# Early MLP-up products, per-tile right-hand sums, later turns and one moved output-projection tile in a two-layer decoder trunk

## The chip, the cores and the metric

One core of a Trainium2 chip runs the whole program in one launch. The metric is device microseconds of that core, the median of several executions. The engines are PE (TensorE), DVE (VectorE), ACT (ScalarE), POOL (GpSimd) and SP (SyncE, which here issues nearly all DMAs). Each takes its instructions in the order of the program.

## The reference

Two layers over 1024 tokens of width 1024, all in f32. Layer 0 mixes with NSA (compressed, selected and window attention), layer 1 with sliding-window attention and sinks (SWA). Each is followed by an MLP; each sublayer is normalised before and after, and modulated by vectors that come from c through `ada_w`.

```python
for i in range(DEPTH):                                   # DEPTH = 2
    mod = silu(c) @ ada_w[i] + ada_b[i]
    sh1, sc1, g1, sh2, sc2, g2 = split(mod, 6)
    h = modulate(rms_norm(x, norm_g[i, 0]), sh1, sc1)
    y = nsa_mixer(h, ...) if i % 2 == 0 else swa_sink_mixer(h, ...)
    x = x + (1 + g1) * rms_norm(y, norm_g[i, 1])
    h = modulate(rms_norm(x, norm_g[i, 2]), sh2, sc2)
    a = relu(h @ w_up)                                   # 1024 -> 4096
    y = (a * a) @ w_down                                 # 4096 -> 1024
    x = x + (1 + g2) * rms_norm(y, norm_g[i, 3])
```

## The kernel before, in words

An f32 product is made of three matmuls (lines 572 to 574): each operand is split into a high part (`wh`, `hh`, `oh`, hi of `wt`; ACT or DVE rounds it) and a low part (`wl`, `hl`, `ol`, lo of `wt`; one subtraction), and hi·hi, lo·hi and hi·lo are added in PSUM.

The order of the work is written out by hand: `spread` interleaves lists of steps, `go` runs them one by one, and after each step lets up to two entries of the list `behind` run whose delay has passed. `later(f, n)` puts an entry there with a delay of n steps, `chain` runs stages one step apart. The first entry holds back those behind it.

**Output projection.** For each of eight token tiles, `out_steps` loads the attention output `o` (in layer 0 two halves from HBM, added by DVE on L1727), splits it into `oh` and `ol`, and runs 48 matmuls; then come the gate, the norm (`yg`, `ms`, `r`, `x`), the store, and the next norm (`junk`, `ms`, `r`, `xr` on L472). `done` puts the turns behind, with a delay of DL = 4 steps. In layer 0 the eight tiles follow the attention; in layer 1 they are spread over the attention units.

**Turns.** `turn` transposes `xr` on PE (L1234), ACT puts it into the right operand `raw` (L1245) with scale and bias. Tiles 0 to 3 fill B11 and B21, tiles 4 to 7 fill B12 and B22 (two tiles of 128 x 2 x 512 each).

**MLP up.** h @ w_up goes by 2 x 2 blocks with 7 products in place of 8 (a Strassen scheme) for each of the 16 column pairs q. Products 1 and 2 need only B11 and B21 as right operands, from tiles 0 to 3; products 6, 5, 7, 3 and 4 need sums over all eight: T1 = B12 - B11, B22 - T1, T3 = B22 - B12 and B21 - (B22 - T1). So products 1 and 2 of the first PAIRS0 = 5 pairs run ahead (10 early products of 12 matmuls) while the last tile is normalised and the sums are made: six 128 x 1024 subtractions on POOL and two on DVE (L1257), then `split` of each right operand (ACT L1250, DVE L1251). `prep` makes the left operand `wt` of a product AHEAD = 3 products before it: hi on ACT (L1330), lo on POOL for the early ones and on DVE for the rest (L1331). The first early loads and preps (`lead`) are spread over the last output-projection tile. `load` takes early columns from the pool `raw`, which has three buffers and also serves the weights of the projections and `adaw`.

**Side work.** The modulation vectors are made by DVE from rows of `ada_w` (L323, one 512 KB load each) as side steps of the MLP and of the projections. The gate of layer 0's MLP, `ada_gate(0, 1)`, is a side of its MLP up.

All big tiles of this part (`hr`, `hh`, `hl`, `wt`, `u`, `x`) come from one pool of 41 slots.

Of the kernel before, what the change touches and what calls it, by code (L numbers as in the profile page):

```python
# [18 lines left out]
P = 128  # L19
# [12 lines left out]
PAIRS0 = 5  # L32
SIDE2 = 40
AHEAD = 3
DL = 4
# [57 lines left out]
class Trunk:  # L93
# [1127 lines left out]
    def up_setup(self, w_up, col):  # L1221
# [36 lines left out]

        def tile(t, xr):
            steps = [lambda c=c: (turn(t, xr, c), put(t, c)) for c in range(2)]  # L1260
            if t == 3:
                steps += [lambda c=c, j=j: split((1, 2)[c], raw[0, c, j]) for c in range(2) for j in range(2)]
            if t == 7:
                V, G = nc.vector, nc.gpsimd
                b11, b21, b12, b22, t1 = (lambda j, n=n: (*n, j) for n in ((0, 0), (0, 1), (1, 0), (1, 1), (2, 0)))
                steps.append(lambda: [minus(e, *f(j)) for f in (lambda j: (t1(j), b12(j), b11(j)), lambda j: (b11(j), b22(j), t1(j)))
                                      for j, e in ((0, V), (1, G))])
                steps += [lambda j=j: (split(6, raw[b11(j)]), minus(G, b12(j), b22(j), b12(j))) for j in range(2)]
                steps += [lambda j=j: (split(5, raw.pop(t1(j))), minus(G, b21(j), b21(j), b11(j)), raw.pop(b11(j))) for j in range(2)]
                for p, b in ((7, b12), (3, b22), (4, b21)):  # L1270
                    steps += [lambda p=p, b=b, j=j: split(p, raw.pop(b(j))) for j in range(2)]
            return steps
# [24 lines left out]
        def prep(i):  # L1297
# [10 lines left out]
            if p == 1:  # L1308
                r = w[11] if early else w[11]
# [21 lines left out]
            (nc.gpsimd if early else nc.vector).tensor_tensor(lo, r, hi.bitcast(F32), op=ALU.subtract)  # L1331
# [3 lines left out]

        def before(i):

            out = []
            n = i + AHEAD
            if 0 <= n < len(order):  # L1340
                out.append(lambda: prep(n))
            out += [lambda q=q: load(q, True) for q in range(2, PAIRS0) if n == 4 * (q // 2) + q % 2 - 3]
            for q in range(n_q):
                if n == at[q] - 2:
# [3 lines left out]
        lead = [lambda q=q: load(q, True) for q in range(2)] + [f for i in range(-AHEAD, 0) for f in before(i)]  # L1348
        return tile, (R, order, before, left, lead)

    def mlp_up(self, up, side, sd, begin):
# [70 lines left out]
        for i, (q, p) in enumerate(order):  # L1422
# [3 lines left out]
            (ramp if i < 2 * PAIRS0 else steps).extend(own)  # L1426
# [205 lines left out]
    def run(self):  # L1632
# [59 lines left out]
        side = self.ada_gate(0, 0) + self.ada_pre(0, 1)  # L1692
# [4 lines left out]
        for l in range(2):  # L1697
# [14 lines left out]
            def done(t, x, take=take, xr=xr):  # L1712
                def turn():
                    for k, f in enumerate(take(t, xr)):
                        self.later(f, DL if k == 0 else 1)
                self.chain(self.norm_stages(x, xr, t) + [turn])

            if l == 0:
# [11 lines left out]
                def more(n):  # L1730
                    return {26: loads[0:1], 27: loads[1:2], 28: loads[2:3], 29: loads[3:5], 30: loads[5:6], 31: loads[6:]}.get(n, [])

                self.nsa_attention(more, parts[-1][1][QN:])
                self.pe = self.w2 = self.Kc = self.Vc = self.cmask = self.fmask = self.gate = None
                outs = [self.out_steps(t, lambda t=t: load(t), src[t], gate, x1[t], done) for t in range(NT)]
                self.mark("wout")
                outs[0][0]()
                for t in range(NT):
                    steps = outs[t][1]
# [51 lines left out]
            side = self.ada_gate(0, 1, True) + self.ada_pre(1, 0, None, True) if l == 0 else self.ada_gate(1, 1, True)  # L1791
# [35 lines left out]
```

## Time and profile before

| | |
|---|---|
| median of 3 runs | 2559.97 us (2558.47 to 2565.79) |
| profiled execution | 2561.28 us; its span 2559.3 us; granted clock 0.972 |
| busy | PE 2396.3 us (94%), DVE 1946.4 (76%), ACT 1397.0 (55%), POOL 1274.1 (50%) |
| instructions on PE | 11974 matmuls |
| out-projection of layer 0 | PE from 793.4 to 888.7 us |
| layer 0's first product after the early ones | 933.70 us |
| layer 1's first product after the early ones | 1959.00 us |

A time in a row of the timeline is the start in the span, then the duration; what stands in brackets is the idle time of that engine before it and what ended that time. PE's matmuls overlap, so their rate is read from start to start.

### The profile page before, as it was taken

The numbers are of one execution on the slowest core, as the hardware profiler recorded it, in microseconds if no ns is written. First come the engines' busy times: TensorE is split into PE (matmuls) and PEld (weight loads), VectorE is DVE, ScalarE is ACT, GpSimd is POOL, SyncE is SP. The second block draws the span as 40 slices with busy tenths as digits, with TensorE's granted clock in tenths as the row PEclk, the third lists the DMA queues.
The fourth block names the chain that finished last, engine by engine and source line by source line (L and its number), as shares of the span: only waits on it lengthen the run. The fifth ranks groups of instructions, "written<-read, shape, count | busy, mean of one in ns | idle before, by whom it ended". The sixth has DMA issues, their size and how long they took to land.

```text
span 2559.3 us, 36576 instructions
## 1 busy us (share of the span) xinstructions
PE 2396.3 (94%) x11974; PEld 1996.3 (78%) x11974; DVE 1946.4 (76%) x3751; ACT 1397.0 (55%) x2959; POOL 1274.1 (50%) x1256
## 2 busy tenths in 40 slices
PE   6989899999998979999999999889787999999997
PEld 4789788888887867778778887767676788888886
DVE  7965479999895579888899777477647876787656
ACT  4632368898983544444444454378765454445433
POOL 4420566565662255334955613477545543494433
PEclk9999999999999989999999999989899999999999
DMA  7367623122227536555988564452223555587754
GB/s 277 116 220 243 215 79 96 39 90 66 72 67 165 148 127 215 197 185 181 359 312 309 203 215 148 124 157 68 65 67 120 201 170 179 179 308 251 228 185 171
DMA packets 237205, 436.08 MB, mean 170 GB/s; under 512 B 19204, under 2 KB 120792, under 8 KB 237016
## 3 DMA queue, kind: packets, MB, share of 16 engines
q1 hardware_dynamic: 208216, 404.39, 47.3%
q0 software_dynamic: 28800, 29.36, 4.7%
q8 instruction: 94, 1.54, 0.2%
q14 instruction: 95, 0.78, 0.1%
HBM read 319.38 MB, written 114.31 MB: 169 GB/s over the span
## 4 chain that ended last, share of the span: by engine, by line
PE 58%; DVE 16%; DMA 10%; issue 6%; POOL 4%; ACT 4%; SPq 1%; DVEq 0%; POOLq 0%; ACTq 0%
PE b L574 14%; PE b L573 14%; PE b L572 14%; PE b L880 5%; PE b L903 5%; PE o L925 4%; DMA adaw<-in_ada_w_dram 3%; DVE wt L1331 2%; DVE p L884 2%; DMA w<-in_mlp_w_up_dram 2%; DMA w<-in_nsa_w_in_dram 1%; DMA wr<-in_mlp_w_down_dram 1%; DVE u L1358 1%; DVE pT L910 1%; DVE ada L323 1%
## 5 line engine op out<-in xcount | busy, mean ns | idle before, releaser
L574 PE MATMUL b<-hh,wt 128*128 128x512 f32 x896 | 350.8, 395 | 25.1 <-POOL wt L1331 21.2
L572 PE MATMUL b<-hh,wt 128*128 128x512 f32 x896 | 354.4, 396 | 9.8 <-ACT wt L1330 9.8
L573 PE MATMUL b<-st,st 128*128 128x512 f32 x896 | 349.5, 390 | 5.4 <-DVE st L1477 5.4
L573 PE MATMUL b<-hl,wt 128*128 128x512 f32 x896 | 352.4, 393 | 0.0
L574 PE MATMUL b<-st,st 128*128 128x512 f32 x896 | 348.3, 389 | 0.0
L572 PE MATMUL b<-st,st 128*128 128x512 f32 x896 | 332.5, 390 | 1.6 <-DVE u L1358 1.6
L888 ACT ACTIVATE p<-p,nm 128x256 f32<-128x256 f32 (+7 forms) x384 | 251.2, 660 | 59.0 <-DVE nm L884 57.8
L1028 POOL TENSOR_SCALAR p<-p,rl,nsam 128x640 f32<-128x640 f32 (+7 forms) x256 | 200.4, 796 | 137.8 <-DVE rl L1026 96.8
L1477 DVE TENSOR_TENSOR st<-sr,st 128x1024 fp32r<-128x1024 f32 (+1 forms) x128 | 193.3, 1510 | 77.5 <-ACT st L1476 76.1
L1403 POOL TENSOR_TENSOR sx<-u,u 128x512 f32<-128x512 f32 x64 | 106.2, 1660 | 273.0 <-ACT u L1371 224.8
L910 DVE TENSOR_TENSOR pT<-b,pT 128x512 fp32r<-128x512 f32 (+1 forms) x334 | 215.4, 657 | 27.6 <-ACT pT L909 27.4
L574 PEld LDWEIGHTS b<-hh,wt 128*128 128x128 f32 x896 | 170.3, 190 | 66.1 <-POOL wt L1331 22.9
L1370 ACT ACTIVATE u<-u 128x512 f32<-128x512 f32 x128 | 80.6, 630 | 244.6 <-DVE u L1358 244.5
L909 ACT ACTIVATE pT<-b 128x512 fp32r<-128x512 f32 (+1 forms) x334 | 187.2, 580 | 43.1 <-PE b L903 36.9
L572 PEld LDWEIGHTS b<-hh,wt 128*128 128x128 f32 x896 | 170.3, 190 | 50.4 <-ACT wt L1330 15.9
L1476 ACT ACTIVATE st<-sr 128x1024 fp32r<-128x1024 f32 (+1 forms) x128 | 122.2, 955 | 158.8 <-PE b L573 104.8
L573 PEld LDWEIGHTS b<-st,st 128*128 128x128 f32 x896 | 168.2, 188 | 42.6 <-DVE st L1477 8.2
L903 PE MATMUL b<-ident,p 128*128 128x128 f32 x1296 | 195.9, 277 | 5.0 <-DVE nm L884 4.1
L1477 DVE TENSOR_TENSOR st<-wr,st 128x1024 fp32r<-128x1024 f32 (+1 forms) x128 | 181.8, 1420 | 20.8 <-ACT st L1476 18.1
L573 PEld LDWEIGHTS b<-hl,wt 128*128 128x128 f32 x896 | 170.0, 190 | 35.0
L572 PEld LDWEIGHTS b<-st,st 128*128 128x128 f32 x896 | 168.2, 188 | 37.3 <-DVE u L1358 2.3
L574 PEld LDWEIGHTS b<-st,st 128*128 128x128 f32 x896 | 168.2, 188 | 34.7
(276 smaller groups left out, 6183.6 us busy)
## 6 DMA issues: line engine op xcount, KB each, us to landing
adaw<-in_ada_w_dram SPq DMA_DIRECT2D x96, 512.0 KB, 4.7
sr<-s SPq DMA_DIRECT2D x96, 512.0 KB, 4.8
wr<-in_mlp_w_down_dram SPq DMA_DIRECT2D x96, 512.0 KB, 6.0
w<-in_mlp_w_up_dram SPq DMA_DIRECT2D x74, 512.0 KB, 4.2
s<-sx SPq DMA_DIRECT2D x64, 512.0 KB, 5.1
x<-x SPq DMA_DIRECT2D x48, 512.0 KB, 4.1
s<-u SPq DMA_DIRECT2D x64, 256.0 KB, 2.1
we<-in_mlp_w_down_dram SPq DMA_DIRECT2D x64, 256.0 KB, 4.0
```

The lines of the kernel that those rows point to most:

```text
L572: mm(out, s[0], m[0], start=first, stop=False)
L573: mm(out, s[0], m[1], start=False, stop=False)
L574: mm(out, s[1], m[0], start=False, stop=last)
L880: self.nc.tensor.matmul(out, q[:, g], k[z], start=z == 0, stop=z == 1)
L888: self.nc.scalar.activation(p, p, AF.Exp, scale=-1.0, bias=nm, accum_out=l)
L903: nc.tensor.transpose(pt[:, g * P:(g + 1) * P], p[:, cols], self.ident)
L909: nc.scalar.activation(x[:, 0, 0:w], pt[:, 0:w], AF.Copy)
L910: nc.vector.tensor_tensor(x[:, 1, 0:w], pt[:, 0:w], x[:, 0, 0:w].bitcast(F32), op=ALU.subtract)
L1028: nc.gpsimd.tensor_scalar(ps[g], ps[g], rl[:, g:g + 1], gate[:, g, b:b + 1], op0=ALU.mult, op1=ALU.mult)
L1403: nc.gpsimd.tensor_tensor(z[n][:, k], x, y, op=op)
L1476: nc.scalar.activation(hi, r, AF.Copy)
L1477: nc.vector.tensor_tensor(lo, r, hi.bitcast(F32), op=ALU.subtract)
```

## The change

1. PAIRS0 goes from 5 to 6: twelve early products. Their right operands are split in `lead`, their left operands by a schedule (`when`) that is ahead of the old one, and their lo is made by DVE. Loads of the early pairs from the fourth on go to slots.
2. T1 and T3 are made for each of tiles 4 to 7 by itself (`near`): two 128 x 2 x 128 subtractions on DVE and two on POOL. Only B22 - T1 (DVE) and B21 - that (POOL) are left for the end.
3. Turns of tiles 0 to 6 come 8 steps later in place of 4 and run one per step; `go` runs the first two entries that are due, wherever they stand.
4. In layer 0 the first output-projection tile stands in the last attention unit.
5. `ada_gate(0, 1)` is a side of the NSA projection (8 more loads and DVE steps there, 8 fewer in MLP up).

```diff
-PAIRS0 = 5
+PAIRS0 = 6
+TURN = 8
@@ go
-                if self.behind and self.behind[0][1] <= 0:
-                    self.behind.pop(0)[0]()
+                due = next((b for b in self.behind if b[1] <= 0), None)
+                if due:
+                    self.behind.remove(due)
+                    due[0]()
@@ up_setup
+        def near(t, j):
+            if t1(j) not in raw:
+                raw[t1(j)] = self.slot("hr", F32, [P, 2, 512])
+            v = lambda n: raw[n][:, :, (t - 4) * P:(t - 3) * P]
+            nc.vector.tensor_tensor(v(t1(j)), v(b12(j)), v(b11(j)), op=ALU.subtract)
+            nc.gpsimd.tensor_tensor(v(b12(j)), v(b22(j)), v(b12(j)), op=ALU.subtract)
...
-            if t == 3:
-                steps += [lambda c=c, j=j: split((1, 2)[c], raw[0, c, j]) for c in range(2) for j in range(2)]
+            if t > 3:
+                steps.append(lambda: (near(t, 0), near(t, 1)))
             if t == 7:
...
+                steps.append(lambda: [minus(V, b11(j), b22(j), t1(j)) for j in range(2)])
+                for p, b in ((6, b11), (5, t1), (7, b12), (3, b22)):
+                    if p == 5:
+                        steps.append(lambda: [minus(G, b21(j), b21(j), b11(j)) for j in range(2)])
+                    steps += [lambda p=p, b=b, j=j: split(p, raw[b(j)]) for j in range(2)]
+                steps += [lambda j=j: split(4, raw[b21(j)]) for j in range(2)]
...
-                r = self.raw_weight(self.raw, w_up, list(range(KT)), 2 * q * P, P)
+                r = self.raw_weight(self.raw if q < 3 else self.slot, w_up, list(range(KT)), 2 * q * P, P)
...
-            (nc.gpsimd if early else nc.vector).tensor_tensor(lo, r, hi.bitcast(F32), op=ALU.subtract)
+            nc.vector.tensor_tensor(lo, r, hi.bitcast(F32), op=ALU.subtract)
...
+        first = at[0]
+        when = lambda i: -1 if i < 3 else (i - 3) // 2 if i < first else max(i - first + 5, i - AHEAD) if i < first + 5 else i - AHEAD
...
+            out = [lambda n=n: prep(n) for n in range(len(order)) if when(n) == i]
+            if i in (0, 1, 2):
+                out += [lambda q=q: load(q, True) for q in (3 + i,) if q < PAIRS0]
...
+        lead = [lambda q=q: load(q, True) for q in range(3)] + [lambda j=j: split(1, raw[b11(j)]) for j in range(2)] + \
+            before(-1) + [lambda j=j: split(2, raw[b21(j)]) for j in range(2)]
@@ mlp_up
-            (ramp if i < 2 * PAIRS0 else steps).extend(own)
+            (ramp if i < 2 * PAIRS0 + 10 else steps).extend(own)
@@ run
-        side = self.ada_gate(0, 0) + self.ada_pre(0, 1)
+        side = self.ada_gate(0, 0) + self.ada_pre(0, 1) + self.ada_gate(0, 1)
...
-                    for k, f in enumerate(take(t, xr)):
-                        self.later(f, DL if k == 0 else 1)
+                    self.later(lambda: self.chain(take(t, xr)), DL if t == NT - 1 else TURN)
...
+                    if n == NT * 4 - 1:
+                        return spread(loads[6:], [outs[0][0], lambda: None, lambda: None] + outs[0][1][:8])
...
-            side = self.ada_gate(0, 1, True) + self.ada_pre(1, 0, None, True) if l == 0 else self.ada_gate(1, 1, True)
+            side = self.ada_pre(1, 0, None, True) if l == 0 else self.ada_gate(1, 1, True)
```

**Place A: PE at the end of layer 0's attention.** PE before (`o` is the attention's output in PSUM, `b` a PSUM bank, `oh` and `ol` the operand of out-projection tile 0):

```order
L925 MATMUL o_9617<-pT_9713,kv_7926 128x512
L925 MATMUL o_9617<-pT_9723,kv_7926 128x512
L572 MATMUL b_9764<-wh_8498,oh_9741 128x512
L573 MATMUL b_9764<-wl_8499,oh_9741 128x512
L572 MATMUL b_9795<-wh_9212,oh_9741 128x512
L573 MATMUL b_9795<-wl_9213,oh_9741 128x512
L574 MATMUL b_9764<-wh_8498,ol_9742 128x512
```

PE now, at the start of the last unit's weighting:

```order
L906 MATMUL b_9689<-ident,p_9545 128x128
L928 MATMUL o_9679<-pT_9640,kv_7754 128x512 x2
L575 MATMUL b_9700<-wh_8475,oh_9652 128x512
L576 MATMUL b_9700<-wl_8476,oh_9652 128x512
L906 MATMUL b_9707<-ident,p_9567 128x128
L906 MATMUL b_9707<-ident,p_9583 128x128
L906 MATMUL b_9723<-ident,p_9567 128x128
L906 MATMUL b_9723<-ident,p_9583 128x128
L906 MATMUL b_9707<-ident,p_9593 128x128
L906 MATMUL b_9723<-ident,p_9593 128x128
L928 MATMUL o_9679<-pT_9663,kv_7754 128x512
L577 MATMUL b_9700<-wh_8475,ol_9653 128x512
```

The 48 matmuls of tile 0 have moved in between the transposes (L906) and the weighting (L928) of the last unit; tile 1's follow directly after the unit.

SP at the same place, before (`o_5`, `o_6`: stores of the attention's output of tiles 5 and 6; `o_0`: the loads for tile 0):

```order
L1122 DMA o_5_2938<-otmp_9427 128x512
L547 DMA w_10471<-in_mlp_w_up_dram 128x8x128
L1122 DMA o_6_2939<-otmp_9619 128x512
L547 DMA w_10487<-in_mlp_w_up_dram 128x8x128
L1726 DMA o_9734<-o_0_2933 64x8x128 x2
L1726 DMA o_9735<-o_0_2933 64x8x128 x2
```

SP now:

```order
L1125 DMA o_5_2984<-otmp_9396 128x512
L1740 DMA o_9645<-o_0_2979 64x8x128 x2
L1740 DMA o_9646<-o_0_2979 64x8x128 x2
L550 DMA w_10522<-in_mlp_w_up_dram 128x8x128
L1125 DMA o_6_2985<-otmp_9668 128x512
L1186 DMA x_9656<-in_x_dram 128x1024
L1171 DMA gbc_9786<-gate_811 128x1024
L550 DMA w_10545<-in_mlp_w_up_dram 128x8x128
L1740 DMA o_9860<-o_1_2980 64x8x128 x2
L1740 DMA o_9861<-o_1_2980 64x8x128 x2
```

The loads of tile 0 stand ahead of the store of `o_6`; those of tile 1 stand behind the load `w_10545`.

**Place B: POOL at the start of layer 0's MLP up.** POOL before (`r` is the norm's factor of a tile, `wt` a left operand, `hr` a right one):

```order
L451 TENSOR_TENSOR r_10661<-ms_10660,mhalf 128x1
L1331 TENSOR_TENSOR wt_10684<-w_10582,wt_10684 128x512
L1257 TENSOR_TENSOR hr_10725<-hr_10424,hr_9919 128x1024
L1257 TENSOR_TENSOR hr_10421<-hr_10432,hr_10421 128x1024
L1257 TENSOR_TENSOR hr_9919<-hr_10435,hr_10725 128x1024
L1257 TENSOR_TENSOR hr_10424<-hr_10435,hr_10424 128x1024
L1257 TENSOR_TENSOR hr_9927<-hr_9927,hr_9916 128x1024
L1331 TENSOR_TENSOR wt_10734<-w_10547,wt_10734 128x512
L1257 TENSOR_TENSOR hr_9930<-hr_9930,hr_9919 128x1024
L1331 TENSOR_TENSOR wt_10780<-w_10582,wt_10780 128x512
```

POOL now:

```order
L1270 TENSOR_TENSOR hr_10441<-hr_10464,hr_10441 128x2x128
L454 TENSOR_TENSOR r_10650<-ms_10649,mhalf 128x1
L454 TENSOR_TENSOR r_10711<-ms_10710,mhalf 128x1
L1270 TENSOR_TENSOR hr_10438<-hr_10461,hr_10438 128x2x128
L1270 TENSOR_TENSOR hr_10441<-hr_10464,hr_10441 128x2x128
L1260 TENSOR_TENSOR hr_10011<-hr_10011,hr_9990 128x1024
L1260 TENSOR_TENSOR hr_10014<-hr_10014,hr_9993 128x1024
L1418 TENSOR_TENSOR sx_11114<-u_10702,u_11014 128x512
```

No `wt` is left on POOL, and of six large subtractions two are left.

**Place C: PE at a turn in layer 1's attention.** PE before (`o`: weighting, L880: scores, L903: transposes of p, `xr`: the normalised tile):

```order
L574 MATMUL b_18653<-wh_17478,ol_18577 128x512
L925 MATMUL o_18649<-pT_18569,V_16476 128x512
L1234 MATMUL b_18666<-ident,xr_18633 128x128 x4
L1234 MATMUL b_18675<-ident,xr_18633 128x128 x4
L880 MATMUL b_18684<-K_16472,qs_18586 128x256 x4
L880 MATMUL b_18685<-K_16472,qs_18586 128x256 x4
L903 MATMUL b_18708<-ident,p_18355 128x128 x4
```

PE now:

```order
L577 MATMUL b_18667<-wh_17492,ol_18591 128x512
L883 MATMUL b_18680<-K_16486,qs_18600 128x256 x4
L883 MATMUL b_18681<-K_16486,qs_18600 128x256 x4
L906 MATMUL b_18704<-ident,p_18351 128x128 x4
L928 MATMUL o_18663<-pT_18583,V_16490 128x512
L1237 MATMUL b_18732<-ident,xr_18647 128x128 x4
L906 MATMUL b_18741<-ident,p_18351 128x128 x4
L928 MATMUL o_18749<-pT_18636,V_16489 128x512 x2
```

Eight score matmuls and four transposes stand ahead of the turn that stood behind it, and the turn's two halves are a step apart.

## Rows read from the trace of the kernel before

**Rows 1.** The page, part 4: shares of the chain that ended last, by engine.
```profile
PE 58%; DVE 16%; DMA 10%; issue 6%; POOL 4%; ACT 4%; SPq 1%; DVEq 0%; POOLq 0%; ACTq 0%
```

**Rows 2.** Stretch of 50 us: busy of each engine, granted clock, DMA share, GB/s.
```profile
900.00:950.00 50.00, 37.12 (x143) 28.64 (x142) 42.46 (x38) 26.25 (x41) 26.76 (x11) 0.86 0.38 120
```

**Rows 3.** Timeline of PE where layer 0's out-projection begins.
```profile
793.36 0.76 PE L572 MATMUL b<-wh,oh 128*128 128x512 f32 x1 [6.76 <-DVE oh L1179]
...
797.76 0.63 PE L574 MATMUL b<-wh,ol 128*128 128x512 f32 x1
798.18 0.63 PE L572 MATMUL b<-wh,oh 128*128 128x512 f32 x1
...
799.38 0.40 PE L573 MATMUL b<-wl,oh 128*128 128x512 f32 x1
799.62 0.39 PE L574 MATMUL b<-wh,ol 128*128 128x512 f32 x1
```

**Rows 4.** Chain of waits before that: start, duration, what.
```profile
782.29 8.77 DMA o<-o
791.19 1.24 DVE o L1727
792.51 0.70 DVE oh L1179
```

**Rows 5.** Timeline of PE at the start of layer 0's MLP up.
```profile
888.67 1.04 PE L1234 MATMUL b<-ident,xr 128*128 128x128 f32 x8
...
917.24 0.80 PE L574 MATMUL b<-hh,wt 128*128 128x512 f32 x1 [9.82 <-POOL wt L1331]
...
933.70 0.50 PE L572 MATMUL b<-hh,wt 128*128 128x512 f32 x1 [1.63 <-ACT wt L1330]
```

**Rows 6.** Timeline of POOL there.
```profile
899.97 14.99 POOL L1257 TENSOR_TENSOR hr<-hr,hr 128x1024 f32<-128x1024 f32 x5 [2.19 <-ACT hr L1245]
```

**Rows 7.** Timeline of DVE, before and in that stretch.
```profile
863.50 2.35 DVE L1251 TENSOR_TENSOR hl<-hr,hh 128x1024 fp32r<-128x1024 f32 x2
...
895.86 0.75 DVE L472 TENSOR_SCALAR xr<-x,r 128x1024 f32<-128x1024 f32 x1 [1.02 <-POOL r L451]
...
910.48 20.11 DVE L1251 TENSOR_TENSOR hl<-hr,hh 128x1024 fp32r<-128x1024 f32 x9 [3.33 <-ACT hh L1250]
```

**Rows 8.** Timeline of PE at the start of layer 1's MLP up.
```profile
1914.89 0.39 PE L572 MATMUL b<-hh,wt 128*128 128x512 f32 x1
...
1942.56 0.80 PE L574 MATMUL b<-hh,wt 128*128 128x512 f32 x1 [9.81 <-POOL wt L1331]
...
1959.00 0.50 PE L572 MATMUL b<-hh,wt 128*128 128x512 f32 x1 [1.64 <-ACT wt L1330]
```

**Rows 9.** Waits of PE from 1700 to 1915: total, times, longest.
```profile
PE b L1234 <- DVE xr L472: 17.1, 5, 5.1
```

**Rows 10.** Timeline of PE at one of these turns.
```profile
1774.16 1.18 PE L1234 MATMUL b<-ident,xr 128*128 128x128 f32 x8 [4.12 <-DVE xr L472]
1774.99 2.06 PE L880 MATMUL b<-K,qs 128*128 128x256 f32 x8
...
1779.40 1.10 PE L880 MATMUL b<-K,qs 128*128 128x256 f32 x8
```

**Rows 11.** Waits of PE from 940 to 1240 (MLP up of layer 0).
```profile
PE b L574 <- DVE wt L1331: 3.3, 3, 2.7
...
PE b L436 <- DVE adag L432: 2.9, 1, 2.9
```

**Rows 12.** Line L323 up to 300 us: durations in ns; what its engine waited for.
```profile
L323 DVE SCALAR_TENSOR_TENSOR ada<-adaw,cond,ada x21: 1264/1285/2316, 77.3 to 265.7; 128x1024 f32<-128x1024 f32 x21
...
  DMA adaw<-in_ada_w_dram: 17.6, 8
```

**Rows 13.** Timeline of PE in the NSA projection.
```profile
156.35 1.19 PE L838 MATMUL b<-phih,nsac 128*128 128x256 f32 x2 [6.96 <-issue]
```

**Rows 14.** The page, part 6: issues of `adaw`, KB each, median us to landing.
```profile
adaw<-in_ada_w_dram SPq DMA_DIRECT2D x96, 512.0 KB, 4.7
```

More of the change, by code (lines that the diff above doesn't have):

```diff
@@ L1257, in minus @@
             eng.tensor_tensor(raw[out], raw[x], raw[y], op=ALU.subtract)
+        b11, b21, b12, b22, t1 = (lambda j, n=n: (*n, j) for n in ((0, 0), (0, 1), (1, 0), (1, 1), (2, 0)))
+        def near(t, j):
[4 more added lines that the diff above has]
+            nc.gpsimd.tensor_tensor(v(b12(j)), v(b22(j)), v(b12(j)), op=ALU.subtract)
         def tile(t, xr):
             steps = [lambda c=c: (turn(t, xr, c), put(t, c)) for c in range(2)]
-            if t == 3:
-                steps += [lambda c=c, j=j: split((1, 2)[c], raw[0, c, j]) for c in range(2) for j in range(2)]
+            if t > 3:
+                steps.append(lambda: (near(t, 0), near(t, 1)))
             if t == 7:
                 V, G = nc.vector, nc.gpsimd
[L1265 to L1271, printed above, removed]
+                steps.append(lambda: [minus(V, b11(j), b22(j), t1(j)) for j in range(2)])
[4 more added lines that the diff above has]
+                steps += [lambda j=j: split(4, raw[b21(j)]) for j in range(2)]
             return steps
@@ L1308, in prep @@
             if p == 1:
-                r = w[11] if early else w[11]
+                r = w[11]
             elif p == 2:
@@ L1334, in prep @@
                 wraw.pop(q)
+        first = at[0]
+        when = lambda i: -1 if i < 3 else (i - 3) // 2 if i < first else max(i - first + 5, i - AHEAD) if i < first + 5 else i - AHEAD
         def before(i):
[L1338 to L1342, printed above, removed]
+            out = [lambda n=n: prep(n) for n in range(len(order)) if when(n) == i]
+            if i in (0, 1, 2):
+                out += [lambda q=q: load(q, True) for q in (3 + i,) if q < PAIRS0]
             for q in range(n_q):
-                if n == at[q] - 2:
+                if i == (2 if q == 0 else when(at[q] - 2)):
                     out.append(lambda q=q: load(q, False))
             return out
-        lead = [lambda q=q: load(q, True) for q in range(2)] + [f for i in range(-AHEAD, 0) for f in before(i)]
+        lead = [lambda q=q: load(q, True) for q in range(3)] + [lambda j=j: split(1, raw[b11(j)]) for j in range(2)] + \
+            before(-1) + [lambda j=j: split(2, raw[b21(j)]) for j in range(2)]
         return tile, (R, order, before, left, lead)
@@ L1730, in more @@
                 def more(n):
-                    return {26: loads[0:1], 27: loads[1:2], 28: loads[2:3], 29: loads[3:5], 30: loads[5:6], 31: loads[6:]}.get(n, [])
+                    if n == NT * 4 - 1:
+                        return spread(loads[6:], [outs[0][0], lambda: None, lambda: None] + outs[0][1][:8])
+                    return {26: loads[0:1], 27: loads[1:2], 28: loads[2:3], 29: loads[3:5], 30: loads[5:6]}.get(n, [])
+                outs = [self.out_steps(t, lambda t=t: load(t), src[t], gate, x1[t], done) for t in range(NT)]
                 self.nsa_attention(more, parts[-1][1][QN:])
-                self.pe = self.w2 = self.Kc = self.Vc = self.cmask = self.fmask = self.gate = None
-                outs = [self.out_steps(t, lambda t=t: load(t), src[t], gate, x1[t], done) for t in range(NT)]
                 self.mark("wout")
-                outs[0][0]()
                 for t in range(NT):
-                    steps = outs[t][1]
+                    steps = outs[t][1][8 * (t == 0):]
                     if t + 1 < NT:
```

## The prediction

> **What bounds the kernel now.** I read the page's chain first [rows 1]: PE holds 58% of it, DVE 16%, DMA 10%. PE is busy 94% of the span, and the change adds and removes no matmul, so time can only come from stretches in which PE waits or runs slowly. The 50 us slices of the busy view find them: around 900 us PE is busy for 37 of 50 us at a granted clock of 0.86 [rows 2]. I then read PE's timeline through each such stretch, and from there the engine that it names. The reader is to see four places. At the start of layer 0's out-projection PE idles 6.76 us for `oh` [rows 3], which follows a chain of loads [rows 4]. At the start of each MLP up PE idles 9.8 us for a `wt` made on POOL [rows 5, 8], because POOL runs five subtractions of 3.0 us in a row first [rows 6]. In layer 1's attention five turns wait 17.1 us for `xr` [rows 9]. In layer 0's MLP up some single waits are left [rows 11].
>
> After a wait PE is also slower for a while: behind the 6.76 us the matmuls start 0.42 us apart (797.76, 798.18), later 0.23 (799.38, 799.62) [rows 3], the two levels of 1.2 and 2.4 GHz. So a removed wait gives back more than itself, and a wait that takes its place costs more than itself.
>
> **The change part by part**, against the profiled execution: 2561.28 us, its span 2559.3 and 2.0 around it. It is 1.3 us above the median of the runs shown, so the forecast is nearly one against either.
>
> *First out-projection tile.* The wait of 6.76 us goes, and with it 13 slow matmuls at 0.2 us each, 2.6: 9.4 us. Tile 0 now needs `oh` inside the last unit. Its loads stand ahead of a store that they stood behind, so the 8.8 + 1.2 + 0.7 us of [rows 4] lie beside the attention. What is late next is tile 1: 48 matmuls at 0.23 are 10.9 us, moved ahead of the attention's end at 786.6 (793.36 less the wait), so that PE wants tile 1 near 797.5. Its loads stand behind `w_10545`, which waits for a buffer, and need the same chain; if they are issued 3 to 8 us after the time at which tile 0's were under way (782.29; an estimate), `oh` is there at 797 to 802. I take 3 us of waiting, 2 of slow clock and 1 inside the unit. Gain 3; bounds 9.4 (nothing late) and -2 (the whole wait comes back at tile 1 and one in the unit).
>
> *Start of MLP up, layer 0.* From the end of the last out-projection matmul (888.67) to the first later product (933.70) pass 45.0 us [rows 5]. In them lie 10 early products of 12 matmuls, 2.73 us each, and two turns of 0.9: 29.1. So 15.9 is waiting and slow clock. Now 12 products stand there; without any wait they and the turns take 34.6. Against 45.0 plus two products (5.5), that is 15.9 less. Two waits come in place. The last tile's turn stands behind 24 matmuls where it stood behind 36: PE is there 6.3 us after 888.67, but `xr` ends 7.9 after it [rows 7], and on DVE one T1 pair and two `wt` now stand in front of it (some 2 us at the width of [rows 7]). So PE waits 1.6 to 4.8 there, and runs slowly behind it for 1 to 2. Everything queued on PE behind that turn waits too, which is why this counts in full. Then DVE has to be through: after `xr` it runs eight `hl` and two B22 - T1 at 1.18 [rows 7], about eight `wt`, four `ws` and four evictions at half that width, 0.6 each, and two T1 parts: 22.4 us, ending 31 after 888.67 if nothing slows it, with PE arriving at 37 to 38. Beside POOL the same `hl` took 2.23 us instead of 1.18 [rows 7]; POOL still has two subtractions of 3 us and four small ones, so DVE may end at 37 to 41 with the waits for ACT's hi. I take 8 us for both waits together, so a gain of 8. Bounds: 15.9 without any wait, 0 if the new waits are as long as the old.
>
> The Trainium skill ("SBUF — State Buffer", section "SBUF: two separate sides") says that the port pair of GpSimd and VectorE "is an exclusive lock, not a bandwidth split", taken by a VectorE operation with two SBUF inputs for the whole instruction. The trace agrees so far that 9 `hl` at 1.18 and POOL's work beside them add up to about the 20.1 us [rows 7]. By that rule it matters little which of the two makes `wt` lo: DVE's 22.4 us and POOL's 8 add up, DVE is through 39 us after the last out-projection matmul, later with the waits for ACT, and the gain is about the 8 taken. If both ran side by side without loss, only the turn would count, and the gain would be 11.
>
> *Start of MLP up, layer 1.* The same edit on the same stretch: 1914.89 to 1959.00 is 44.1 us [rows 8], with one turn inside; 15.9 is waiting and slow clock again. Gain 8, bounds 0 and 15.9.
>
> *Gate out of MLP up.* The wait for `adag`, 2.9 us, goes with its steps; DVE has 8 steps of 1.28 fewer [rows 12] in a stage whose first part has DVE busy for 42 of 50 us [rows 2], which may take away the 3.3 us of waits for `wt` as well [rows 11]. Gain 4, bounds 2 and 7.
>
> *Turns in layer 1's attention.* The five waits are 17.1 us [rows 9]. Now eight scores, four transposes and one weighting stand ahead of the turn: scores 1.1 us, or 2.1 at the slow clock [rows 10], four transposes half of a turn's 1.2, so about 2.4 in all. Of five waits with 17.1 in sum and 5.1 the longest, two are near 1.5 and three between 4 and 5.1; each loses up to 2.4: 10. The scores themselves may wait for their loads in some places. I take 8; bounds 14 (POOL's `r`, now ahead of its other work, brings `xr` sooner too) and 0 (PE meets the next wait instead).
>
> *Gate into the NSA projection.* Eight steps of 1.28 us, and DVE waited 17.6 us for `adaw` in 21 steps [rows 12], 0.84 each: some 17 us more on DVE, which is not full there. It reaches PE where PE waits for DVE: in the stretch before L838 with its 6.96 us [rows 13] stand several of them now. I take a quarter: 4 us lost. Bounds: 12 lost, 3 gained (a shifted load that falls better).
>
> *The rest* (right operands of products 1 and 2 split in `lead`, one more early load, T1 and T3 inside the out-projection) lies beside out-projection matmuls where PE has not waited; without that cover its four extra splits cost 4 x 1.2. I count 0.
>
> Sum: 3 + 8 + 8 + 4 + 8 - 4 = 27. 2561.3 - 27 = 2534 us.
>
> **The rivals.** *DVE becomes the bound of the early products.* It has T1, the `wt` and all `hl`, in order, each behind an hi of ACT. For it: 2.23 us beside POOL, and nine `hl` in 20.1 us already. Against it: POOL has 14.99 us less to do there. Then each MLP-up start gains 2 or 3 rather than 8: 2534 + 11 = 2545.
>
> *All waits go.* 9.4 + 15.9 + 15.9 + 4 + 10 - 4 = 51: 2510. For it: none of the covers needed is longer than what stands beside it by much. Against it: the turn's position, which is behind 24 matmuls in both layers.
>
> *The projection pays for everything (slower).* `adaw` shares three buffers with the weights, and DVE takes its steps in order. If PE has to wait out each of the 8 extra loads and its step, at 4.7 us to landing [rows 14] and 1.28, that is 48; less the other gains, 31: 2578. It decides from 31 / 8 = 3.9 us per step. For it: PE's 6.96 us stand next to such a step. Against it: DVE's mean wait is 0.84 us a step, and PE has weights and products of other columns in that stage.
>
> *The moved tile changes nothing*: tile 1 takes over the wait in full. That is 3 less, 2537, inside the forecast.
>
> **How the numbers follow.** The forecast has 0.62: its terms are off by some 4, 5, 5, 2, 5 and 6 us, together about 11, so its own range is 2519 to 2549. DVE as the bound 0.19 (2538 to 2556), all waits gone 0.10, the projection 0.05, other losses that leave the time near before 0.04. Leaving out half of the "all gone" case and the slower ones gives 2512 to 2556. A measurement tells 0.3% from no change, 7.7 us: faster is below 2552.3, slower above 2567.6. Faster: nearly all of the first, two thirds of the second, all of the third, 0.82. Slower: the projection and part of the rest, 0.07. Same: 0.11.
>
> **What would show it.** In the changed profile PE's wait for `oh` at tile 0 is gone, and one of up to 5 us stands at tile 1. At both MLP-up starts no row waits for a POOL `wt`; the last tile's turn waits 2 to 5 us for `xr`; the first product after twelve early ones starts some 42 us after the last out-projection matmul. The five turns of layer 1's attention wait 7 to 9 us in place of 17. The NSA projection is 4 us longer. I am wrong if DVE is busy without a gap from `xr` to that product while PE waits for `hl` or `wt` for 8 us or more, or if the projection grows by over 12 us.

## The result, and the profile after

The changed kernel takes 2591.52 us (median of 4 runs, 2588.66 to 2594.18); its ratio to the kernel before is 1.0115, 95% interval 1.0094 to 1.0136. The forecast was 2534, with a range of 2512 to 2556: wrong in sign, by 57 us. The span of the profiled execution is 2591.3 us, 32.0 longer than before, with as many matmuls. Where the time went is seen first from the lengths of the stages; their borders are the starts of the first or last matmul of a kind in PE's timeline (first score against the compressed keys; last out-projection matmul; last lo·hi product of MLP up; last of MLP down; first score of layer 1).

| stage | before, us | after, us | difference | forecast |
|---|---|---|---|---|
| setup and NSA projection | 302.4 | 312.1 | +9.7 | +4 |
| NSA attention and out-projection | 586.0 | 599.4 | +13.4 | -3 |
| MLP up, layer 0 | 341.3 | 332.7 | -8.6 | -12 |
| MLP down, layer 0 | 324.7 | 355.1 | **+30.4** | no term |
| layer 1's projection | 97.2 | 97.7 | +0.5 | 0 |
| layer 1's attention and out-projection | 263.0 | 254.8 | -8.2 | -8 |
| MLP up, layer 1 | 325.6 | 318.8 | -6.8 | -8 |
| MLP down, layer 1 | 305.9 | 307.1 | +1.2 | 0 |

Three stages gained, together 24 us of the 28 forecast for them. Three others lost 54: one with the right sign in the forecast and less than half the size, one with the wrong sign, and one without a term.

**The gains.** PE's timeline at the start of layer 0's MLP up, after (it answers to [rows 5]):

```profile
911.48 0.40 PE L577 MATMUL b<-wh,ol 128*128 128x512 f32 x1
...
924.57 1.97 PE L1237 MATMUL b<-ident,xr 128*128 128x128 f32 x8 [6.31 <-DVE xr L475]
...
955.52 0.39 PE L575 MATMUL b<-hh,wt 128*128 128x512 f32 x1
```

The wait of 9.8 us for POOL's `wt` is gone; the last tile's turn now waits 6.3 for `xr`. The thirteenth product starts 44.0 us after the last out-projection matmul; before it took 52.7, in the same count. DVE and POOL there, after (to [rows 6, 7]):

```profile
938.61 5.69 DVE L1254 TENSOR_TENSOR hl<-hr,hh 128x1024 fp32r<-128x1024 f32 x3
...
950.11 2.35 DVE L1254 TENSOR_TENSOR hl<-hr,hh 128x1024 fp32r<-128x1024 f32 x2
```
```profile
934.75 6.20 POOL L1260 TENSOR_TENSOR hr<-hr,hr 128x1024 f32<-128x1024 f32 x2
```

The first of the three `hl` alone is this row:

```profile
938.61 3.42 DVE L1254 TENSOR_TENSOR hl<-hr,hh 128x1024 fp32r<-128x1024 f32 x1
```

It took 3.42 us and ended 1.1 us after POOL's second subtraction (934.75 + 6.20); the two behind it, with POOL idle, took 1.21 each. From `xr` to the thirteenth product DVE is busy nearly without a gap, but PE waits only 0.4 us for it. Later in this MLP up it does, from 958 to 1260 (to [rows 11]); the wait for `adag` is gone:

```profile
PE b L577 <- DVE wt L1343: 8.8, 5, 4.2
```

Layer 1, PE, after (to [rows 8]):

```profile
1951.80 0.39 PE L577 MATMUL b<-wh,ol 128*128 128x512 f32 x1
...
1960.17 1.97 PE L1237 MATMUL b<-ident,xr 128*128 128x128 f32 x8 [2.53 <-DVE xr L475]
...
1989.76 0.39 PE L575 MATMUL b<-hh,wt 128*128 128x512 f32 x1
```

The 9.8 us are gone here too; 38.0 us to the thirteenth product, against 50.2 before. The turns in layer 1's attention, waits of PE from 1745 to 1951 (to [rows 9]):

```profile
PE b L1237 <- DVE xr L475: 14.5, 6, 4.0
```

Their sum fell only from 17.1 to 14.5 us, though the stage is 8.2 shorter; part of the rest came from other waits of that stage (PE's 5.8 us for `pT` are gone).

**The losses.** Start of the attention, PE before, where nothing stood but a wait for the q loads, and then after:

```profile
302.39 1.94 PE L1033 MATMUL b<-nsac,qs 128*128 128x64 f32 x8 [6.42 <-DMA qs<-qd]
```
```profile
304.71 0.29 PE L352 MATMUL b<-adas,fold 128*32 128x8 f32 x8 [7.04 <-DVE adas L348]
306.25 0.38 PE L439 MATMUL b<-ident,adag 128*8 128x128 f32 x1 [1.24 <-DVE adag L435]
312.07 1.97 PE L1036 MATMUL b<-nsac,qs 128*128 128x64 f32 x8 [5.44 <-DMA qs<-qd]
```

It is mostly the end of the moved gate, not its eight steps: PE's last product ahead of it ends 1.7 us later than before, and `adaw` cost DVE 14.5 us of waiting in 28 steps, less than before in 21 [rows 12].

The out-projection tile in the last unit, PE after (to [rows 3]), ACT, and SP:

```profile
800.66 0.47 PE L575 MATMUL b<-wh,oh 128*128 128x512 f32 x1 [2.58 <-DVE oh L1182]
...
826.32 0.56 PE L575 MATMUL b<-wh,oh 128*128 128x512 f32 x1 [4.51 <-DVE oh L1182]
```
```profile
804.15 0.60 ACT L912 ACTIVATE pT<-b 128x512 fp32r<-128x512 f32 x1 [5.13 <-PE b L906]
```
```profile
813.73 0.38 SPq L550 DMA_DIRECT2D w<-in_mlp_w_up_dram  x1
814.20 1.22 SPq L1740 DMA_DIRECT2D o<-o  x2
```

Tile 0 still waits, now in the middle of the unit, so that the unit's own transposes (L906) come late for ACT. Tile 1 waits as well, since its loads stand behind a `w` that SP could issue only at 813.7.

MLP down of layer 0. SP's waits from 1490 to 1530, then DVE and ACT there, after:

```profile
SPq L1796 <- DVE x L525: 27.2, 1, 27.2
```
```profile
1500.07 0.69 DVE L1492 TENSOR_TENSOR st<-wr,st 128x512 fp32r<-128x512 f32 x1
1513.30 5.21 DVE L1510 TENSOR_TENSOR y<-b,y 128x512 f32<-128x512 f32 x8 [12.55 <-PE b L577]
```
```profile
1496.84 0.61 ACT L1491 ACTIVATE st<-wr 128x512 fp32r<-128x512 f32 x1
1516.75 0.63 ACT L516 ACTIVATE junk<-y 128x512 bf16<-128x512 f32 x1 [19.29 <-DVE y L1510]
```

Between 1501 and 1513 ACT, DVE and POOL do nothing and SP issues no load. ACT (`junk`), POOL (`r`) and SP (the store of `x`) each hold an instruction of the first output tile's norm, DVE the additions into `y` that this norm needs; all wait for products that PE is still at. The operands (`sr`, `wr`, `st`) of the products after those are queued behind. In SP's queue as the program has it, the store of that tile's `x` stands ahead of the loads:

```
L1791 DMA x_15378<-x_0_0_2971 128x1024
L1796 DMA x_0_10658<-x_15378 128x1024
L1454 DMA sr_15427<-s_5_10684 128x512
L1458 DMA wr_15428<-in_mlp_w_down_dram 128x512
```

In the kernel before no such store stands there. PE has single waits from 1526 on, and behind them runs at the lower level for parts of two stretches (granted clock 0.67 in 1530 to 1540, 0.66 in 1550 to 1560; in the kernel before 1.00 in every stretch from 1490 to 1570). The waits of PE over the whole stage, before and after, are

```profile
PE b L573 <- DVE st L1477: 4.6, 6, 1.2
```
```profile
PE b L576 <- DVE st L1492: 8.6, 5, 2.7
PE b L491 <- DVE xr L475: 7.2, 2, 5.3
```

and some single ones: 6.2 us in 7 waits before, 19.6 in 13 after. Busy time (PE with its count of matmuls first), granted clock and DMA of the stage, before and after:

```profile
1229.80:1554.60 324.80, 318.55 (x1434) 261.01 (x1433) 279.11 (x256) 150.86 (x192) 165.23 (x91) 1.00 0.74 264
```
```profile
1244.20:1599.30 355.10, 335.39 (x1455) 272.34 (x1454) 283.42 (x257) 151.78 (x194) 166.83 (x92) 0.97 0.68 245
```

So 13.4 of the 30.4 us are waits. The 21 matmuls more belong to layer 1's projection and now stand ahead of the last products; at 0.23 us each they are 4.8. The granted clock of 0.97 means, as an estimate, that 6% of the stage, some 21 us, ran at the lower level and lost half of that, about 10.

### The profile page after: what moved, and what is told of

Read it like the earlier page. It is cut to its first block, busy times and chain, and to the rows that moved or that the text cites. A ratio compares the mean times of both kernels' runs of the same rounds, so it can differ in the third digit from the quotient of the medians.

```text
span 2591.3 us, 36633 instructions
## 1 busy us (share of the span) xinstructions
PE 2411.3 (93%) x11974; PEld 2003.6 (77%) x11974; DVE 1984.7 (77%) x3787; ACT 1393.9 (54%) x2959; POOL 1236.4 (48%) x1244
## 5 line engine op out<-in xcount | busy, mean ns | idle before, releaser
L576 PEld LDWEIGHTS b<-st,st 128*128 128x128 f32 x896 | 170.0, 190 | 47.9 <-DVE st L1492 12.5
L906 PE MATMUL b<-ident,p 128*128 128x128 f32 x1296 | 196.9, 275 | 10.3 <-POOL p L1031 5.3
L1492 DVE TENSOR_TENSOR st<-wr,st 128x1024 fp32r<-128x1024 f32 (+1 forms) x128 | 187.3, 1463 | 20.7 <-ACT st L1491 16.2
L575 PEld LDWEIGHTS b<-st,st 128*128 128x128 f32 x896 | 169.7, 190 | 40.4 <-ACT st L1491 3.7
L577 PEld LDWEIGHTS b<-st,st 128*128 128x128 f32 x896 | 170.2, 190 | 35.3
```

Source lines behind the costliest of these rows:

```text
L575: mm(out, s[0], m[0], start=first, stop=False)
L576: mm(out, s[0], m[1], start=False, stop=False)
L577: mm(out, s[1], m[0], start=False, stop=last)
L906: nc.tensor.transpose(pt[:, g * P:(g + 1) * P], p[:, cols], self.ident)
L1492: nc.vector.tensor_tensor(lo, r, hi.bitcast(F32), op=ALU.subtract)
```

## The experiments

Each ratio is against executions of the kernel before that were measured together with that run (medians of 2559.0 to 2562.2 us).

| label | what | median, us | ratio to the kernel before, interval |
|---|---|---|---|
| e1_head | changed, old rule of `go` | 2567.17 | 1.0029 (1.0020 to 1.0038) |
| e2_gate | changed, gate back in MLP up | 2584.72 | 1.0097 (1.0082 to 1.0112) |
| e3_tile0 | changed, tile 0 after the attention | 2578.31 | 1.0074 (1.0059 to 1.0089) |
| e4_three | all three of these undone | 2544.60 | 0.9943 (0.9924 to 0.9962) |
| e5_go_alone | before, new rule of `go` | 2587.68 | 1.0112 (1.0099 to 1.0125) |
| e6_head_down | changed, old rule in MLP down only | 2563.11 | 1.0004 (0.9995 to 1.0014) |
| e12_store_pool | changed, store of x issued by POOL | 2589.82 | 1.0111 (1.0096 to 1.0127) |
| e15_two_pool | e12, gate row too | 2588.30 | 1.0103 (1.0085 to 1.0120) |
| e14_wl_first | changed, `wl` ahead of tile 0 | 2599.46 | 1.0152 (1.0138 to 1.0166) |
| e8_ramp | e4, side steps sooner | 2551.80 | 0.9971 (0.9960 to 0.9982) |
| e9_turn4 | e4, TURN = 4 | 2548.07 | 0.9956 (0.9943 to 0.9968) |
| e11_turn_split | e4, delay 4 in layer 0, 8 in layer 1 | 2545.72 | 0.9943 (0.9931 to 0.9956) |
| e10_lo_pool | e4, early lo on POOL | 2559.31 | 1.0000 (0.9990 to 1.0010) |
| e16_lo_alone | before, early lo on DVE | 2554.75 | 0.9969 (0.9957 to 0.9982) |
| e13_pairs5 | e4, five early pairs | 2537.27 | 0.9914 (0.9900 to 0.9927) |
| e17_pairs56 | e4, five pairs in layer 0, six in layer 1 | 2537.43 | 0.9904 (0.9891 to 0.9918) |

**The three losses, one by one and together.**

```diff
# e1_head
-                due = next((b for b in self.behind if b[1] <= 0), None)
+                if self.behind and self.behind[0][1] <= 0:
# e2_gate
-        side = self.ada_gate(0, 0) + self.ada_pre(0, 1) + self.ada_gate(0, 1)
+        side = self.ada_gate(0, 0) + self.ada_pre(0, 1)
...
-            side = self.ada_pre(1, 0, None, True) if l == 0 else ...
+            side = self.ada_gate(0, 1, True) + self.ada_pre(1, 0, None, True) if l == 0 else ...
# e3_tile0
-                    if n == NT * 4 - 1:
-                        return spread(loads[6:], [outs[0][0], ...] + outs[0][1][:8])
+                    return {26: ..., 31: loads[6:]}.get(n, [])
...
+                outs[0][0]()
...
-                    steps = outs[t][1][8 * (t == 0):]
+                    steps = outs[t][1]
```

> The changed kernel with the old rule of go (only the head of the list behind may run). Theory: under the new rule the store of the first finished tile of layer 0's MLP stands on SP ahead of the last loads of MLP down, SP waits 27 us there and starves ACT, DVE and PE; with the old rule the store stands behind the loads again, the SP wait of 27 us is gone, and the time is about 2591 - 27 = 2564 us. The turns of layer 1's attention keep their gain, because it comes from the delay of 8. Rival: the loss comes from the larger set of slots held (six pairs), so the order of the store is a symptom: then the time stays within 5 us of 2591.

> The changed kernel with the gate of layer 0's MLP back as a side of MLP up. Theory: its end (transposes on DVE, a PE step that waits 7 us for them) stands at the head of the attention and costs about 12 us there; without it the attention starts 12 us earlier, MLP up pays about 3 again: 2591 - 9 = 2582 us, with PE's wait for adas gone. Rival: the eight extra loads and DVE steps inside the projection are what costs: then the gain shows already at 150 to 250 us, and not at 300. Second rival: the wait for the q loads that stands there anyway takes all of it: 2591.

> The changed kernel with the first output-projection tile after the attention again. Theory: tile 0 inside the last unit loses more than the 9.4 us that it saves, because its loads are issued late and the loads of tile 1 wait on SP behind a weight load until 814 us; without it the out-projection ends about 15 us earlier: 2576 us. Rival: the last units are late for another reason (the sixth pair's load and the early splits): then the 9.4 us come back as a loss, 2600 us.

> The changed kernel with all three undone (go's rule, the gate, tile 0), so with six pairs, sums per tile and later turns. Theory: the three losses are apart from one another and add up, 27 + 9 + 15: about 2540 us, faster than the kernel before by some 20 us, which is what the two MLP-up starts and the turns of layer 1's attention gave. Rival: they overlap (one wait hides another), and the time is near the kernel before, 2560 us.

Measured: 24 us less (MLP down of layer 0 325.1 us, as before the change), 7 less (the attention starts at 299.6, PE's wait for `adas` gone), 13 less (attention and out-projection 588.0 us), and 47 less together; the three alone add up to 44. The losses add up, and without them the rest of the change is 0.57% faster than the kernel before. The 7 us of e2 are the least sure, since the intervals of e2 and of the changed kernel overlap, and its trace does not put them at the gate: the attention starts 12.5 us earlier, MLP up of layer 0 is 11.9 longer (344.6 us), and it is MLP down that is shorter, by 8.8 (346.3). So at its two ends the move comes out at nothing; why MLP down gains is not shown. The turns of layer 1's attention kept their gain under the old rule (253.7 us), so it is not `go` that brought it.

**The rule alone, and where it costs.** e5 puts the new rule into the kernel before; e6 keeps it in the changed kernel everywhere but in MLP down.

> The kernel before with one edit alone: go's new rule (first two entries that are due), and the two halves of a turn as a chain with the old delay of 4, which the rule needs so that they keep their order. Theory: the rule by itself puts the store of the first finished tile ahead of the last loads on SP, and costs what undoing it gave back: 2560 + 24 = 2584 us, lost between 1490 and 1560. Rival: it costs that only together with six pairs and the gate in the projection: 2560.

> The changed kernel with the old rule of go inside MLP down alone; everywhere else the first due entry runs. Theory: the rule costs only where the post-norm chains of layer 0's first output tiles overtake the entries with long delays, so this gives the same as the old rule everywhere: 2567 us. Rival: the rule also costs in the out-projection or the starts of MLP up, and this stays above 2575.

e5: 28 us slower, MLP down of layer 0 at 354.1 us. e6: as fast as e1 or a little faster, MLP down at 328.8. So the rule costs by itself, and, by the whole time, in MLP down and nowhere else.

**Which queue holds the work up.** Two edits take SP's early entries away, with go's rule as it is:

```diff
# e12_store_pool
-                    nc.sync.dma_start(xd[t], x)
+                    (nc.gpsimd if l == 0 else nc.sync).dma_start(xd[t], x)
# e15_two_pool: as e12, and in ada_gate's put
+                (nc.gpsimd if (l, which) == (1, 0) else nc.sync).dma_start(...)
```

> The changed kernel as it is, with one edit: the store of x at the end of layer 0's MLP is issued by POOL and not by SP. Go's rule and the order on the other engines stay. Theory: what costs is SP alone, which waits 27 us for x with the loads of MLP down behind it; then those loads flow and about 20 of the 24 us come back: 2591.5 - 20 = 2571 us. Rival: the new rule costs through DVE or PE, which meet yg, ms and the turns too early; then the time stays near 2588.

> The changed kernel with both early entries of SP's queue in layer 0's MLP down issued by POOL: the store of x and the row of the next layer's gate, which took the store's place as SP's wait (20.3 us) when only the store was moved. Theory A: SP was the only holder, its loads now flow, and 20 us come back: 2570 us. Theory B: the chain of the first tile is early on every queue; ACT's statistics of y (junk, which waited 19 us for DVE's y) stand ahead of the rounding of the next operands (st), so ACT holds the work up as well, and the time stays near 2588.

My theory that SP's store alone is the cause fell: with it on POOL, SP waits for the gate's row instead (e12's waits, 1485 to 1560); with both gone, ACT still waits as long as before (e15's waits, 1480 to 1560).

```profile
SPq L442 <- ACT row L441: 20.3, 1, 20.3
```
```profile
ACT junk L516 <- DVE y L1510: 19.3, 1, 19.3
```

MLP down stays at 351.2 and 350.0 us. Clearing SP is worth at most 4 to 5 of the 30 us by these two traces, and nothing clear of noise by the times. What is left is the chain of the first tile on the other queues, ACT's `junk` above all, as theory B has it. That is argued from what remains: no run holds the norm back on ACT or on DVE alone.

**Tile 0 with its weights first.**

```diff
-                        return spread(loads[6:], [outs[0][0], ...] + outs[0][1][:8])
+                        return loads[6:] + [outs[0][0], ...] + outs[0][1][:8]
```

> The changed kernel with one edit: in the last attention unit the last weight step of the out-projection (wh, wl) stands ahead of tile 0's steps and is not spread between them. Theory: wl ended at 813.7 us on POOL, SP held the load w_10545 for it and behind that the loads of tile 1; with wl some 10 us earlier tile 1 no longer waits 4.5 us for oh and slowly behind it: 2591.5 - 7 = 2584 us. Rival: tile 0's matmuls hold up the unit's own transposes on PE, and that is the whole of the 13 us that the tile cost: 2590.

Worse by 8 us, though it did what it was to do: SP issues the `w` at 803.7 and tile 1 no longer waits for `oh`. But tile 0's loads are later, and PE and ACT of e14 read:

```profile
808.55 0.77 PE L575 MATMUL b<-wh,oh 128*128 128x512 f32 x1 [6.82 <-DVE oh L1182]
```
```profile
810.70 0.60 ACT L912 ACTIVATE pT<-b 128x512 fp32r<-128x512 f32 x1 [8.33 <-PE b L906]
```

In these two runs the longer wait of tile 0's first matmul inside the unit (2.58, then 6.82 us) goes with the longer wait of ACT for the unit's transposes behind it (5.13, then 8.33), and attention and out-projection grow from 599.4 to 605.5 us. This speaks for the rival of this run; how the 13 us that the tile cost are made up in full stays open.

**What carried the gain.** In e4, three single edits: side steps directly after the early products (the diff holds them back for ten products more, which the list of the change does not name), the shorter turn delay, the early lo on POOL; e11 has the delay of 4 in layer 0 only; e16 has the lo on DVE as the one edit of the kernel before.

```diff
# e8_ramp
-            (ramp if i < 2 * PAIRS0 + 10 else steps).extend(own)
+            (ramp if i < 2 * PAIRS0 else steps).extend(own)
# e9_turn4 (e11: only where l == 0)
-TURN = 8
+TURN = 4
# e10_lo_pool; e16_lo_alone is the reverse, in the kernel before
-            nc.vector.tensor_tensor(lo, r, hi.bitcast(F32), op=ALU.subtract)
+            (nc.gpsimd if early else nc.vector).tensor_tensor(lo, r, hi.bitcast(F32), op=ALU.subtract)
```

> The last kernel (three parts undone, 2544.6 us) with side steps beginning after the twelve early products, and not ten products later. Theory: in that kernel layer 0's MLP up gives back some 9 us of what its start gained, because 48 side steps of DVE are pressed into ten products fewer; with the old beginning PE's waits for DVE's wt there (16.2 us in ten) halve: 2538 us. Rival: DVE is full at the start, so that the first later product comes later by as much: 2545 to 2550.

> The kernel with three parts undone, with TURN = 4 in place of 8. Theory: the later place of the turn in PE's order is what gained 11 us in layer 1's attention (from +4.5 to -6.3 us against the kernel before); with 4 the turns wait again: 2554 us. Rival: the halves a step apart do it, or sooner r on POOL: 2545.

> The kernel with three parts undone, with the delay of 4 for the turns of layer 0 and of 8 for those of layer 1. Theory: each layer keeps its better half: with 4 everywhere layer 0 reached its thirteenth product 39.1 us after the out-projection instead of 44.4, and layer 1's attention lost 4 us; so about 2544.6 - 6 = 2538 us. Rival: the 5 us of layer 0 are given back in its MLP up, where DVE is full: 2545.

> The kernel with three parts undone, with the lo of the twelve early left operands on POOL again. Theory: DVE and POOL hold each other up, so the engine of these 0.6 us subtractions matters little: within 4 us of 2544.6, with DVE's hl longer again. Rival 1: DVE is the bound at both starts, so that taking 12 x 0.6 us from it gains 5 us in each layer: 2535. Rival 2: POOL's long subtractions hold up wt as in the kernel before: 2555.

> The kernel before with one edit alone: the lo of the ten early left operands on DVE. In the kernel with three parts undone, taking this one back cost 15 us, all that it had gained. Theory: PE's waits of 9.8 us for a wt behind POOL's long subtractions go in both layers, and the time falls to about 2548; what is left is DVE's hl beside POOL's subtractions. Rival: without sums per tile DVE and POOL are both full there, hl ends later by the ten lo, and the time stays at 2558.

e8 is 7 us slower, with intervals that just touch, so the late start of the side steps is more likely right than not. e9 and e11 are not told apart from e4 by their intervals. With the delay of 4 layer 0 is faster to its thirteenth product (38.9 us in e9 against 44.2, counted as above), and its whole MLP up is 8 us shorter (334.2 and 333.7 against 342.3). In e9 layer 1's attention is slower by 4 (256.8 against 252.6); in e11, split between the layers, the other stages of the trace are 0.7 to 2.1 us longer each, and no gain was left to measure. With the delay of 4 layer 1's attention still is 6 us shorter than the 263.0 before, so the later turn brings some 4 of the gain there; which other part brings the rest was not told apart. e10 is the clear one: lo on POOL takes back all that e4 had gained, 15 us. POOL's timeline in e10 shows four `wt` in a row where e4 has none:

```profile
904.24 5.86 POOL L1341 TENSOR_TENSOR wt<-w,wt 128x512 fp32r<-128x512 f32 x4
```

and its early products end late in both layers (thirteenth product 48.7 and 39.0 us after the out-projection, e4 44.2 and 35.7). That is 8 of the 15 us; the others, in the later part of layer 1's MLP up and in its attention (256.4 against 252.6), were not traced to a wait. e16 gives 0.31% by that edit alone; PE's waits from 885 to 1240 in it read

```profile
PE b L574 <- DVE wt L1331: 15.4, 6, 7.4
```

so the lo moved from behind POOL's subtractions into DVE's line of `hl`: one long wait went, a shorter one came. Only with the sums per tile does it also go.

**The sixth pair.** In e4 the start of layer 0's MLP up gains 8.5 us, but the whole of it takes 342.3 us against 341.3 before: all given back.

```diff
# e13_pairs5 (e17: in layer 0 only)
-PAIRS0 = 6
+PAIRS0 = 5
```

> The kernel with three parts undone, with five early pairs in place of six. Theory: most of the gain at the MLP-up starts comes from wt and sums leaving POOL, but ten early products (27 us) are over before DVE has its eight hl: PE waits some 4 us more in layer 0 and 2 in layer 1, 2550 us. Rival: the sixth pair costs slots and loads and gives nothing: 2541.

> The kernel with three parts undone, with five early pairs in layer 0 and six in layer 1. Theory: with six pairs layer 0's MLP up gives back the 8.5 us that its start gained (342.3 us from the out-projection to its end against 332.3 with five), because its 48 DVE side steps fall on fewer products; layer 1 with 24 is 3.5 us shorter with six. So 2537.3 - 3.5 = 2534 us. Rival: layer 1's difference is not steady, and this is the same as five in both, 2537.

The theory of e13 fell: five pairs are faster by 7 us. PE's waits over layer 0's MLP up, first in e4, then in e13:

```profile
PE b L575 <- DVE wt L1341: 16.2, 10, 3.8
```
```profile
PE b L575 <- DVE wt L1341: 5.6, 5, 2.4
```

With six pairs and 48 side steps (24 loads and 24 operations on DVE) PE waits for `wt` three times as long; MLP up is 332.3 us with five pairs. In the changed kernel, where the gate is elsewhere and 32 side steps are left, six pairs keep the gain (332.7). The loss lies behind the start: from the thirteenth product to its end MLP up takes 288.6 us in the kernel before and in the changed one, 287.5 in e13, but 298.1 in e4 and 300.8 in e2. So it comes with the sixth pair and the gate together. It is not that the steps have fewer products to fall on, as the expectations have it: e8 gives them ten products more and takes 302.4 us there. Whether the two contend for DVE's time or for slots was not told apart. Layer 1 is 1 to 4 us shorter with six pairs, and e17 has the lowest ratio, 0.9904, but it and e13 are one by their intervals. Both beat the kernel before and the changed one.

## Why the prediction was wrong

- **A term was missing.** The sum goes through the tile, the starts, the gate and the turns, and counts "the rest" at 0. The rule of `go`, part of the third listed edit, has no term at all. It cost 24 to 28 us (e1, e5, e6), about half of the error of 57. The tile is another 16 (gain 3 forecast, 13 lost), the gate some 7 (0 forecast), and what is left in e4 gained 15 us, where the two starts and the turns were to bring 24. The trace of before could not show it as a wait, because in the program the old rule hid the conflict: an entry with a long delay at the head of `behind` held the norms of the first output tiles back until the operands of the last products were queued. It was to be seen in the program's order: the store of `x` ahead of the loads `sr` and `wr` on SP.
- **"First out-projection tile: gain 3"** failed in sign; it lost 13 (e3). Its reason, that tile 0's loads lie beside the attention, failed: tile 0 waited 2.58 us, inside the unit. The forecast counted 1 us for that and nothing for what stands behind it on PE. Tile 1's wait (4.5 us and a slow stretch) came as forecast, but with SP held until 813.7.
- **"Gate into the NSA projection: 4 lost"** had the right sign, and its place was wrong: the eight steps cost little (1.7 us by PE's last product), and with the end of the gate (transposes on DVE, a PE step, the transpose of the row) it is 9.7 at the head of the attention, where PE has nothing else. "Gate out of MLP up: gain 4" was too small beside six pairs: with the gate back there e2's MLP up is 11.9 us longer. The two ends of the move cancel, as the sum had it, at three times the size.
- **The two MLP-up starts (8 and 8)** were right in mechanism: no wait for POOL's `wt` is left, `xr` is the new wait (6.3 and 2.5 us; forecast 2 to 5), and to the thirteenth product 8.7 and 12.2 us are gained. The stages kept 8.6 and 6.8. That layer 0 would have given it all back with the gate in place (e4) was not foreseen.
- **"The rest: 0"** was too small as well. In e4, where tile 0 stands after the attention as before, the out-projection of layer 0 takes 100.5 us from its first matmul to its last, and 97.2 to 101.1 in the variants of e4; before it took 95.1. In e4 PE has two new waits there, 1.0 and 1.5 us, for `ms`.
- **The weighing of one engine against the other.** From the exclusive lock that the Trainium skill states ("SBUF — State Buffer", section "SBUF: two separate sides") I concluded that the choice of engine for lo matters little, since both engines' times add up. The slowed `hl` beside POOL (3.42 us, then 1.21 alone) agrees with the lock; the conclusion that I drew did not hold. Nor does the sum that I took from [rows 7] come out of the row as it stands: POOL is busy 16.1 of those 20.1 us, and nine `hl` at 1.18 are 10.6 more; how much of POOL's time was waiting the row does not tell. e10 and e16 give 15 and 7 us for the choice. The sum of the two engines is not what PE waits for: it waits for one `wt`, and behind five subtractions of 3 us that comes late [rows 5, 6].
- **The turns (8)** came to 8.2, by other waits than I named: the `xr` waits fell by 2.6 us, not by 8 to 10, and by e9 the later place brings some 4 us. That the number fits is luck.
- **The rivals.** None was right. The slower one named the projection (48 us by the loads); the slowdown came from elsewhere. DVE as the bound of the starts did not show: PE waits 0.4 us for DVE in the changed kernel's start of layer 0, and of the 16.2 us in e4 15.1 lie behind the thirteenth product, where the rival did not look.

## What to carry to other kernels

A change to the rule that orders deferred work has to be priced over the whole program, also in stages that its author did not have in mind: list where the order of each in-order queue changes, and look for an entry that waits long and has now moved ahead of loads. Moving work into the middle of an attention unit can bring its waits with it, and since PE takes its instructions in the program's order they hold up all that stands behind. And a gain at the start of a stage is only a gain if its end is read too: with a side load on the same engine it can be handed back within the stage.

## What the runs showed of the hardware

Waits of PE cost more than they last. In MLP down of layer 0 they are 13.4 us longer than before, and the stage is 30.4 longer; 4.8 of the rest are matmuls of the next stage. Behind the wait of 2.17 us at 1531 matmuls start 0.43 us apart, before it 0.23, and the granted clock of that stretch of 10 us is 0.67; how the rest is shared between the clock and the changed order is the estimate above and was not measured apart. On DVE one 128 x 1024 subtraction `hl` took 1.21 us with POOL idle and 2.2 to 3.4 while POOL was at a subtraction of the same size, in the kernel before and in the changed one.
